# Gate sums of a Mamba-2 mixer: parts made at once, one logarithm, exponential and pair of scalings per group

## The chip, the cores and the metric

The kernel runs on one core of a Trainium2 chip. The core has a matrix engine (TensorE, in the profile PE, with its weight loads as PEld), a vector engine (DVE), an activation engine (ACT), a general engine (POOL) and a queue engine (SP) that issues the transfers. Each engine works through its own list of instructions in order and waits on semaphores. The metric is device time in microseconds; lower is better. Three runs of the kernel before took 2956.16 to 2961.75 us, median 2960.67.

## The reference

One inference step of a hybrid decoder: a Mamba-2 layer, a window-attention layer, each with an MLP, over 1024 prompt rows, 64 sample rows and 16 meta rows (T = 1104 columns here). The change touches the gated norm behind the Mamba-2 scan:

```python
def gated_group_rmsnorm(y, z, w):
    g = (y * jax.nn.silu(z)).astype(jnp.float32)
    shp = g.shape
    g = g.reshape(shp[:-1] + (N_GROUPS, shp[-1] // N_GROUPS))
    g = g * lax.rsqrt(jnp.mean(g * g, axis=-1, keepdims=True) + EPS)
    return (g.reshape(shp) * w.astype(jnp.float32)).astype(y.dtype)
...
    zxbcdt = rmsnorm(h, norm_w) @ w_in
    z = zxbcdt[..., :D_INNER]
...
    out = gated_group_rmsnorm(y, z, gate_w) @ w_out
```

There are 8 groups of 256 features. Each needs z (a product of the normed stream with 256 columns of w_in), the gate, the mean square over its 256 features, its inverse root, and the scaling by that and by w.

## The kernel before

Everything is kept features by rows: 128 partitions hold 128 features, the free dimension runs over the 1104 rows, cut into three chunks of 384, 384 and 336 columns (CH). A group is two tiles of 128 features. Products in full precision are made as three products of rounded parts (mm3, L199 to L206): a number is split into a rounded high part (an ACT copy) and the rest (a subtract).

`gate_group` (L740) makes the gates of one group. It loads two units of weights (wunit, L156: load, ACT cast L170, POOL subtract L171) and the scan's y. For each chunk it makes two products of 24 matrix instructions each; each lands in a bank of PSUM (the matrix engine's output memory; seven banks in this stage). ACT takes the tanh (L754), DVE makes z(1 + tanh) (L755), POOL multiplies by y (L762), ACT squares (L763), DVE adds the two squares (L764). The squares lie in a tile g2 with tag n3, of which there are two.

The sum over the 256 features runs across partitions, so it is a product with a matrix of ones: `sum_over` (L239) splits g2's sum into hi and lo (L249, L250; tiles of tag n1, five of them), multiplies both with ones into one bank (L251, L254) and returns it; `rstd` (L257) takes logarithm (L262) and exponential (L263) of it on ACT, which is the inverse root. `gate_norm` (L776) calls this with rs = the second half of g2, and scales y's two tiles chunk by chunk (L783). After the third chunk `side_sums` (L794) makes sums and differences of the group's quarters on DVE (L800) and stores them (L801, L815) for the block products; groups 6 and 7 are stored as they are (L792).

`gate_norm` isn't called where a chunk's sum is ready. It is put in a list `due` with a count of 3, and `tick` counts down once per product: right after it is put there, after the first product of the next chunk, and after its second. So it is called when the next chunk's products have been written out. Its first product with ones is held behind all matrix instructions written before it (keep_in_program_order, L253). The rest of the order on each engine is fixed at build time by a scheduler that works from its own estimate of times and puts first what it believes ready.

Group 0's gates run inside the last group's scan, groups 1 to 7 in `gates_out` (L822), where one unit of later weights is also split ahead after each group (`split_ahead`, L842: load, split, two stores). When the gates are done, `block_products` (L1216) multiplies the gates with the output weights, in steps p (4 column blocks) and i (7 products each); its raw weights lie in tiles of tag raw for even p and n3 for odd p (L1141). The last chunk of group 7 is still due then: `more` (L855) ticks at p = 0, i = 3 and i = 6, with the ones product in a bank of the block products.

Of the kernel before, what the change touches and what calls it, by code (L numbers as in the profile page):

```python
# [8 lines left out]
F32 = mybir.dt.float32  # L9
F32R = mybir.dt.float32r  # L10
AF = mybir.ActivationFunctionType
ALU = mybir.AluOpType
# [4 lines left out]
P = 128  # L17
D = 1024
# [7 lines left out]
T = META + NM  # L26
# [3 lines left out]
G = 8  # L30
# [12 lines left out]
KB = 3  # L43
# [50 lines left out]
class Stream:  # L94
# [29 lines left out]
    def load(self, X):  # L124

        self.X = X
        for c in self.rs:
            self.k.nc.sync.dma_start(out=X[:, :, self.cols(c)], in_=self.h_d[:, :, self.cols(c)])
        for c in list(self.rs):
            self.norm(c)  # L130
# [11 lines left out]
class Kernel:  # L142
# [96 lines left out]
    def sum_over(self, ssum, n, pin=False):  # L239


        nc = self.nc
        if self.pstat is None:
            ms = self.gps()
        else:
            ms = self.pstat[0].tile([P, self.pstat[3] if len(self.pstat) > 3 else 512], F32, tag=self.pstat[1],
                                    bufs=self.pstat[2], name="ms")
        hi, lo = (self.np.tile([P, 384], F32R, tag="n1", bufs=5, name="ms" + p)[:, :n] for p in "hl")
        nc.scalar.copy(out=hi, in_=ssum)  # L249
        nc.vector.tensor_tensor(out=lo, in0=ssum, in1=hi.bitcast(F32), op=ALU.subtract)  # L250
        a = nc.tensor.matmul(out=ms[:, :n], lhsT=self.ones_r, rhs=hi, start=True, stop=False)  # L251
        if pin:
            self.tc.keep_in_program_order(a)  # L253
        nc.tensor.matmul(out=ms[:, :n], lhsT=self.ones_r, rhs=lo, start=False, stop=True)  # L254
        return ms[:, :n]
# [484 lines left out]
    def gate_group(self, g, xs, y, gt, tmp):  # L740


        nc, i = self.nc, self.i
        w = [self.wunit(self.in_tile(2 * g * P + j * P), KT, P) for j in range(2)]
        for j in range(2):
            nc.sync.dma_start(out=y[j], in_=self.y_d[g][:, j])
        for c, (o, n) in enumerate(CH):
            yv = [t[:, o:o + n] for t in y]
            g2 = gt(c)[:, :, :n]
            for j in range(2):  # L750
                pt = self.gps()
                self.mm3(pt[:, :n], [(w[j][0][:, k], w[j][1][:, k]) for k in range(KT)],
                         [(xs[c][0][:, k, :n], xs[c][1][:, k, :n]) for k in range(KT)])
                nc.scalar.activation(out=g2[:, j], in_=pt[:, :n], func=AF.Tanh, scale=0.5)  # L754
                nc.vector.scalar_tensor_tensor(out=g2[:, j], in0=g2[:, j], scalar=1.0, in1=pt[:, :n],  # L755
                                               op0=ALU.add, op1=ALU.mult)
                if j == 0:
                    self.tick()
                    yield

            for j in range(2):
                nc.gpsimd.tensor_tensor(out=yv[j], in0=g2[:, j], in1=yv[j], op=ALU.mult)  # L762
                nc.scalar.activation(out=g2[:, j], in_=yv[j], func=AF.Square)  # L763
            nc.vector.tensor_tensor(out=g2[:, 0], in0=g2[:, 0], in1=g2[:, 1], op=ALU.add)  # L764
            self.due.append([3, partial(self.gate_norm, g, c, y, g2, tmp)])
            self.tick()
            yield

    def tick(self, n=1):
# [3 lines left out]
        while self.due and self.due[0][0] <= 0:  # L773
            self.due.pop(0)[1]()

    def gate_norm(self, g, c, y, g2, tmp):  # L776
        nc = self.nc
        o, n = CH[c]
        rs = self.rstd(g2[:, 0], n, self.eps4, D / 256, g2[:, 1], pin=True)
        for j in range(2):  # L780
            ft = 2 * g + j
            yv = y[j][:, o:o + n]
            nc.vector.scalar_tensor_tensor(out=yv, in0=yv, scalar=self.nv[:, ft % 8, 6 + ft // 8:7 + ft // 8], in1=rs,  # L783
                                           op0=ALU.mult, op1=ALU.mult)
        if c < 2:
            return
        if g < 2 * KB:
            self.side_sums([t[:, i * T // 2:(i + 1) * T // 2] for t in y for i in range(2)],
                           self.rz[g // KB][:, :, :, g % KB], tmp(), tmp())
        else:  # L790
            for j in range(2):
                nc.sync.dma_start(out=self.gd[g][:, j], in_=y[j])  # L792
# [24 lines left out]
    def gate_of(self, g, xs, yps):  # L817
        y = yps[g % 2].tile([P, 2, T], F32, tag="y", bufs=1, name="gy")
        return self.gate_group(g, xs, [y[:, 0], y[:, 1]], lambda c: self.n3(),
                               lambda: yps[0].tile([P, T // 2], F32, tag="m", bufs=2, name="gm"))  # L820

    def gates_out(self, xs, big, cr, co, cb, yps, gate):  # L822

        nc = self.nc
        nn = T // 2
        ya = yps[1]
        for c, (o, n) in enumerate(CH):
            nc.sync.dma_start(out=big[:, :, o:o + n], in_=self.i["x"][:, :, o:o + n])
        R0 = self.R0 = self.pool("R0", ctx=self.cR, right=True).tile([P, 2, 4, T], F32R, name="R0")
        slot = [P, 2, KB, nn]  # L830
        A5 = self.pool("A5", ctx=co, right=True).tile(slot, F32R, name="A5")
        size = 2 * KB * nn
        cut = lambda t, n: [t[:, k * size:k * size + size].rearrange("p (e q n) -> p e q n", e=2, q=KB)
                            for k in range(n)]
        S = cut(self.S.rearrange("p e k n -> p (e k n)"), 5)
        B = cut(R0.rearrange("p e k n -> p (e k n)"), 2)
        slots = [[[(t[:, 0], t[:, 1])] for t in ts] for ts in ([A5] + B + S[:4], [S[4], A5, A5] + S[:4])]
        load, parts = self.side_io(self.rz, slots)
        for g in range(1, G):
            for _ in gate if g == 1 else self.gate_of(g, xs, yps):  # L840
                pass
            self.split_ahead()  # L842
            if g == 4:
                for i in range(3):
                    load(0, i)
            if g in (5, 6):
                for i in ((0,), (1, 2))[g - 5]:
                    parts(0, i)
        cr.close()
        for i in range(3, 7):  # L850
            load(0, i)
        cb.close()
        us = self.pool("us", ctx=co).tile([P, 4, nn], F32, name="us")

        def more(b, p, i):  # L855
            if (b, p) != (0, 0):
                return
            if 1 <= i <= 4:
                parts(0, i + 2)
            if i in (3, 6):  # L860

                self.pstat = (self.pq, self.CHAIN[0][3], 1, 1024)
                self.tick(2 if i == 3 else 9)
                self.pstat = None
            if i == 6:

                t = ya.tile([P, 4, nn], F32R, tag="y", bufs=1, name="A6")
                rest = self.S.rearrange("p e k n -> p (e k n)")[:, 5 * size:].rearrange("p (q n) -> p q n", q=2)
                slots[1][1] = [(rest, t[:, 0:2]), (t[:, 2:3], t[:, 3:4])]
        self.pq = self.pool("pq", space=PSUM, ctx=co)  # L870
        rd = [self.gd.get(g) for g in range(G)]
        self.block_products(self.i["w_outs"], big, us, slots, load, parts, [(0, 3, 4, 5, 6)], [(3, 6, 7, 8, 10)],
                            (lambda: self.block_load(rd, 3, R0), lambda j: self.block_parts(j, R0)), more, (1, 1))

    def out_last(self, hts, done, norm):
# [1134 lines left out]
```

## Time and profile before

| | |
|---|---|
| runs, median (lowest to highest) | 2960.67 us (2956.16 to 2961.75) |
| the profiled execution | 2959.25 us |
| its span, first to last instruction | 2957.5 us |
| mean granted TensorE clock | 0.982 |
| busy: PE, PEld, DVE | 2829.4, 2719.1, 1888.0 us |
| busy: ACT, POOL | 1454.4, 1370.7 us |
| moved by DMA | 433.44 MB, mean 147 GB/s |

The page's shares are over the whole span; the change is in a stretch of about 300 us (the gates, roughly 600 to 880 us, and the first block products behind them), so that stretch is what has to be read. Busy times of PE are modelled (matrix instructions overlap), so idle time and the pace of products say more than the share. In rows of the order of time the columns are start, duration, engine, line, operation, output<-inputs, shape and count, with the idle time before it and what ended that in brackets. In the list of waits a row has total us, times and the longest.

### The profile page before, as it was taken

To read this page: it belongs to the slowest core of one execution; us is meant where nothing else is said; L and a number is where in the kernel's file an instruction comes from. 1 tells how busy PE (TensorE), PEld (TensorE's weight loads), DVE (VectorE), ACT (ScalarE), POOL (GpSimd) and SP (SyncE) were. 2 spreads that over 40 slices of the span, in tenths; PEclk is the share of its full clock that TensorE was granted. 3 is DMA by queue.
4 is the path that set the end of the run, shared out by engine and by line. 5 is a ranking of instruction groups with operands and counts; after the bars stand their busy time and mean duration, and the time that the engine had idled before them with its cause. 6 is when DMAs were issued, how large, how long until landed. Compare 5 with 4: busy or idle time off the path is not lost.

```text
span 2957.5 us, 51821 instructions
## 1 busy us (share of the span) xinstructions
PE 2829.4 (96%) x19895; PEld 2719.1 (92%) x19895; DVE 1888.0 (64%) x3027; ACT 1454.4 (49%) x2782; POOL 1370.7 (46%) x1279
## 2 busy tenths in 40 slices
PE   8999999989888999999999999999999999999997
PEld 6998999979888999999999999988889999999997
DVE  6788777764645766454547765665678554366675
ACT  6555555556664355545433425555555444433333
POOL 5466666664444714444356663312111444335562
PEclk9999999999998999999999999999999999999999
DMA  3344444447553233444645522447454343543422
GB/s 135 97 131 120 123 125 122 130 136 262 190 199 123 97 113 116 150 140 154 240 166 188 177 79 75 161 152 263 145 187 152 131 156 130 196 161 123 143 99 75
DMA packets 219471, 433.44 MB, mean 147 GB/s; under 512 B 30728, under 2 KB 128392, under 8 KB 216648
## 3 DMA queue, kind: packets, MB, share of 16 engines
q1 hardware_dynamic: 219224, 430.14, 43.7%
q8 instruction: 156, 2.56, 0.4%
q14 instruction: 91, 0.75, 0.1%
HBM read 302.71 MB, written 128.32 MB: 146 GB/s over the span
## 4 chain that ended last, share of the span: by engine, by line
PE 59%; DVE 7%; ACT 4%; issue 4%; DMA 3%; POOL 3%; SPq 0%; DVEq 0%; ACTq 0%; POOLq 0%
PE g L204 6%; PE g L206 6%; PE g L205 6%; PE mc L204 4%; PE mc L205 3%; PE mc L206 3%; PE ma L204 3%; PE ma L205 3%; PE ma L206 3%; PE md L206 3%; PE md L205 3%; PE mb L204 3%; PE mb L206 3%; PE md L204 3%; PE mb L205 3%
## 5 line engine op out<-in xcount | busy, mean ns | idle before, releaser
L1031 POOL TENSOR_TENSOR w<-s,w 128x384 fp32r<-128x384 f32 (+1 forms) x272 | 364.8, 1347 | 421.7 <-ACT w L1030 386.0
L204 PE MATMUL g<-S,w 128*128 128x384 f32 (+2 forms) x1584 | 535.2, 338 | 2.2 <-ACT w L170 0.8
L206 PE MATMUL g<-S,w 128*128 128x384 f32 (+2 forms) x1584 | 532.8, 337 | 3.4 <-POOL w L171 2.7
L205 PE MATMUL g<-S,w 128*128 128x384 f32 (+2 forms) x1584 | 535.2, 338 | 0.0
L1031 POOL TENSOR_TENSOR w<-raw,w 128x384 fp32r<-128x384 f32 (+1 forms) x204 | 262.1, 1290 | 278.5 <-ACT w L1030 247.7
L171 POOL TENSOR_TENSOR w<-raw,w 128x1024 fp32r<-128x1024 f32 x96 | 243.8, 2541 | 273.6 <-ACT w L170 211.8
L206 PEld LDWEIGHTS g<-S,w 128*128 128x128 f32 x1584 | 303.7, 192 | 5.2 <-POOL w L171 3.0
L204 PEld LDWEIGHTS g<-S,w 128*128 128x128 f32 x1584 | 302.9, 191 | 5.9 <-issue 1.6
L205 PEld LDWEIGHTS g<-S,w 128*128 128x128 f32 x1584 | 303.7, 192 | 0.9 <-issue 0.3
L1030 ACT CAST w<-s 128x384 fp32r<-128x384 f32 (+1 forms) x272 | 150.0, 557 | 302.4 <-DVE s L1155 70.6
L204 PE MATMUL ma<-S,w 128*128 128x276 f32 (+1 forms) x808 | 236.2, 292 | 9.3 <-DVE us L1247 6.7
L205 PE MATMUL ma<-S,w 128*128 128x276 f32 (+1 forms) x808 | 235.5, 292 | 2.3 <-DVE S L1213 2.3
L206 PE MATMUL ma<-S,w 128*128 128x276 f32 (+1 forms) x808 | 235.6, 292 | 0.0
L1030 ACT CAST w<-raw 128x384 fp32r<-128x384 f32 (+1 forms) x204 | 112.2, 556 | 161.9 <-PE md L206 46.1
L594 DVE SCALAR_TENSOR_TENSOR fm<-xp,cv,fm 128x1024 f32<-128x1024 f32 x96 | 161.2, 1681 | 33.0 <-ACT fm L575 32.4
L204 PEld LDWEIGHTS ma<-S,w 128*128 128x128 f32 x808 | 154.4, 191 | 10.8 <-ACT w L1030 4.8
L205 PE MATMUL g<-R,w 128*128 128x384 f32 (+2 forms) x480 | 158.3, 330 | 0.0
L204 PE MATMUL g<-R,w 128*128 128x384 f32 (+2 forms) x480 | 157.8, 329 | 0.0
L206 PE MATMUL g<-R,w 128*128 128x384 f32 (+2 forms) x480 | 157.7, 329 | 0.0
L205 PEld LDWEIGHTS ma<-S,w 128*128 128x128 f32 x808 | 154.6, 191 | 2.5 <-DVE S L1213 2.5
L206 PEld LDWEIGHTS ma<-S,w 128*128 128x128 f32 x808 | 154.2, 191 | 0.0
L204 PE MATMUL mc<-S,w 128*128 128x276 f32 (+1 forms) x512 | 149.5, 292 | 4.7 <-DVE rx L1060 2.4
(491 smaller groups left out, 8679.3 us busy)
## 6 DMA issues: line engine op xcount, KB each, us to landing
raw<-in_w_up_dram SPq DMA_DIRECT2D x64, 512.0 KB
raw<-in_w_in_dram SPq DMA_DIRECT2D x48, 512.0 KB
raw<-in_w_downs_dram SPq DMA_DIRECT2D x64, 384.0 KB
w<-ws_o SPq DMA_DIRECT2D x48, 512.0 KB
w<-ws_q SPq DMA_DIRECT2D x40, 512.0 KB
ab<-acs_d SPq DMA_DIRECT2D x64, 256.0 KB
S<-t_d SPq DMA_DIRECT2D x18, 828.0 KB
S<-t_e SPq DMA_DIRECT2D x18, 816.0 KB
```

The costliest lines, as they stand in the source:

```text
L171: nc.gpsimd.tensor_tensor(out=wl, in0=raw, in1=wh.bitcast(F32), op=ALU.subtract)
L204: mm(out=out, lhsT=wh, rhs=xh, start=(first and k == 0), stop=False)
L205: mm(out=out, lhsT=wh, rhs=xl, start=False, stop=False)
L206: mm(out=out, lhsT=wl, rhs=xh, start=False, stop=(k == n - 1))
L594: nc.vector.scalar_tensor_tensor(out=acc[:, :SEQ], in0=xp[:, k:k + SEQ], scalar=cv[:, j, k:k + 1], in1=acc[:, :SEQ], op0=ALU.mult, op1=ALU ...
L1030: nc.scalar.copy(out=t[:, 0], in_=src)
L1031: nc.gpsimd.tensor_tensor(out=t[:, 1], in0=src, in1=t[:, 0].bitcast(F32), op=ALU.subtract)
```

## The change

- `sum_over` is cut in two: `sum_parts` makes hi and lo, `sum_of` makes the products with ones.
- `gate_group` calls `sum_parts` right where a chunk's sum is ready, after the tick, and puts `gate_norm` in the list with a count of 2, without a tick behind it; so the products with ones still come when the next chunk's products have been written out. For group 0's first two chunks it is called at once.
- `gate_norm` copies the sums of a chunk into its columns of one rs tile for the group (ACT). After the third chunk there is one logarithm, one exponential and two scalings over all 1104 columns. The halves of rs serve `side_sums` as its two temporary tiles.
- That tile is the only one of its tag, in the pool that stays open over the block products; before there were two half-wide ones in the other pool.
- After the last group nothing is split ahead. The unit is split later, in the first MLP's block products (L1189).
- The last chunk's tick in the block products is at i = 5, not 3; the tick at i = 6 goes.

```diff
     def sum_over(self, ssum, n, pin=False):
+        return self.sum_of(self.sum_parts(ssum, n), n, pin)
+
+    def sum_parts(self, ssum, n):
+        nc = self.nc
+        hi, lo = (self.np.tile([P, 384], F32R, tag="n1", bufs=5, name="ms" + p)[:, :n] for p in "hl")
+        nc.scalar.copy(out=hi, in_=ssum)
+        nc.vector.tensor_tensor(out=lo, in0=ssum, in1=hi.bitcast(F32), op=ALU.subtract)
+        return hi, lo
+
+    def sum_of(self, parts, n, pin):
...
-        hi, lo = (self.np.tile([P, 384], F32R, tag="n1", bufs=5, name="ms" + p)[:, :n] for p in "hl")
-        nc.scalar.copy(out=hi, in_=ssum)
-        nc.vector.tensor_tensor(out=lo, in0=ssum, in1=hi.bitcast(F32), op=ALU.subtract)
+        hi, lo = parts
...
             nc.vector.tensor_tensor(out=g2[:, 0], in0=g2[:, 0], in1=g2[:, 1], op=ALU.add)
-            self.due.append([3, partial(self.gate_norm, g, c, y, g2, tmp)])
             self.tick()
+            parts = self.sum_parts(g2[:, 0], n)
+            self.due.append([2, partial(self.gate_norm, g, c, y, parts, tmp)])
+            if g == 0 and c < 2:
+                self.tick(2)
             yield
...
-        rs = self.rstd(g2[:, 0], n, self.eps4, D / 256, g2[:, 1], pin=True)
+        if c == 0:
+            self.grs = tmp()
+        rs = self.grs
+        nc.scalar.copy(out=rs[:, o:o + n], in_=self.sum_of(parts, n, g > 0 or c == 2))
+        if c < 2:
+            return
+        nc.scalar.activation(out=rs, in_=rs, func=AF.Ln, bias=self.eps4, scale=D / 256)
+        nc.scalar.activation(out=rs, in_=rs, func=AF.Exp, scale=-0.5)
         for j in range(2):
             ft = 2 * g + j
-            yv = y[j][:, o:o + n]
-            nc.vector.scalar_tensor_tensor(out=yv, in0=yv, scalar=self.nv[:, ft % 8, 6 + ft // 8:7 + ft // 8], in1=rs,
-                                           op0=ALU.mult, op1=ALU.mult)
-        if c < 2:
-            return
+            nc.vector.scalar_tensor_tensor(out=y[j], in0=y[j], scalar=self.nv[:, ft % 8, 6 + ft // 8:7 + ft // 8],
+                                           in1=rs, op0=ALU.mult, op1=ALU.mult)
...
-                           self.rz[g // KB][:, :, :, g % KB], tmp(), tmp())
+                           self.rz[g // KB][:, :, :, g % KB], rs[:, :T // 2], rs[:, T // 2:])
...
-                               lambda: yps[0].tile([P, T // 2], F32, tag="m", bufs=2, name="gm"))
+                               lambda: yps[1].tile([P, T], F32, tag="m", bufs=1, name="gm"))
...
-            self.split_ahead()
+            if g < G - 1:
+                self.split_ahead()
...
-            if i in (3, 6):
+            if i == 5:
                 self.pstat = (self.pq, self.CHAIN[0][3], 1, 1024)
-                self.tick(2 if i == 3 else 9)
+                self.tick(9)
                 self.pstat = None
```

More of the change, by code (lines that the diff above doesn't have):

```diff
@@ L774, in tick, with gate_norm @@
             self.due.pop(0)[1]()
-    def gate_norm(self, g, c, y, g2, tmp):
+    def gate_norm(self, g, c, y, parts, tmp):
         nc = self.nc
         o, n = CH[c]
-        rs = self.rstd(g2[:, 0], n, self.eps4, D / 256, g2[:, 1], pin=True)
+        if c == 0:
[6 more added lines that the diff above has]
+        nc.scalar.activation(out=rs, in_=rs, func=AF.Exp, scale=-0.5)
         for j in range(2):
             ft = 2 * g + j
-            yv = y[j][:, o:o + n]
-            nc.vector.scalar_tensor_tensor(out=yv, in0=yv, scalar=self.nv[:, ft % 8, 6 + ft // 8:7 + ft // 8], in1=rs,
-                                           op0=ALU.mult, op1=ALU.mult)
-        if c < 2:
-            return
+            nc.vector.scalar_tensor_tensor(out=y[j], in0=y[j], scalar=self.nv[:, ft % 8, 6 + ft // 8:7 + ft // 8],
+                                           in1=rs, op0=ALU.mult, op1=ALU.mult)
         if g < 2 * KB:
             self.side_sums([t[:, i * T // 2:(i + 1) * T // 2] for t in y for i in range(2)],
-                           self.rz[g // KB][:, :, :, g % KB], tmp(), tmp())
+                           self.rz[g // KB][:, :, :, g % KB], rs[:, :T // 2], rs[:, T // 2:])
         else:
```

## The prediction

> **What bounds the kernel now.** I read the page first (share of each engine), then the list of waits of PE for the stretch where the gates run, then busy time by stage, then the order of time of one group.
>
> ```profile
> span 2957.5 us, 51821 instructions
> ...
> PE 2829.4 (96%) x19895; PEld 2719.1 (92%) x19895; DVE 1888.0 (64%) x3027; ACT 1454.4 (49%) x2782; POOL 1370.7 (46%) x1279
> ```
> ```profile
> PE ms L254 <- DVE msl L250: 15.2, 8, 3.0
> PE mb L204 <- ACT w L1030: 7.8, 1, 7.8
> PE ms L251 <- ACT msh L249: 11.0, 9, 3.0
> ...
> PE ma L205 <- DVE S L1213: 2.3, 1, 2.3
> ...
> PE g L251 <- ACT msh L249: 2.1, 1, 2.1
> PE ma L204 <- ACT S L1212: 1.3, 1, 1.3
> ```
> ```profile
> 661.40:877.30 215.90, 192.48 (x1050) 186.47 (x1050) 112.14 (x155) 142.10 (x206) 100.30 (x67) 0.94 0.59 210
> 877.30:925.00 47.70, 31.89 (x187) 30.07 (x187) 29.07 (x36) 27.41 (x40) 17.91 (x14) 0.79 0.50 185
> 925.00:980.00 55.00, 53.89 (x419) 53.19 (x418) 39.25 (x43) 24.27 (x34) 33.66 (x26) 1.00 0.45 154
> ```
>
> TensorE is the bound, so only what makes it wait is worth time. The second fence (600 to 960 us) says who makes it wait there: the products with ones (L251, L254) wait for the two parts of a chunk's sum (ACT copy L249, DVE subtract L250). The third fence holds the gates of groups 1 to 7, the entry into the block products, and a quiet stretch to compare with; columns are PE, PEld, DVE, ACT, POOL busy, granted clock, DMA share, GB/s. ACT is busy 142.10 of 215.90 us: not the bound.
>
> How much PE loses, from the pace of its products:
>
> ```profile
> L204 PE MATMUL g<-S,w 128*128 128x384 f32 x224 | 78.7, 351 | 0.0
> ...
> L204 PE MATMUL g<-S,w 128*128 128x336 f32 x112 | 36.1, 322 | 0.0
> ```
> ```profile
> 721.33 0.34 PE L206 MATMUL g<-S,w 128*128 128x384 f32 x1
> ...
> 730.46 0.33 PE L204 MATMUL g<-S,w 128*128 128x384 f32 x1
> ...
> 773.54 0.31 PE L204 MATMUL g<-S,w 128*128 128x336 f32 x1
> ...
> 780.79 0.32 PE L206 MATMUL g<-S,w 128*128 128x336 f32 x1
> ...
> 786.85 0.69 PE L254 MATMUL ms<-msl,ones_r 128*128 128x384 f32 x1 [2.33 <-DVE msl L250]
> 787.34 0.52 PE L205 MATMUL g<-S,w 128*128 128x384 f32 x1
> 787.66 0.52 PE L206 MATMUL g<-S,w 128*128 128x384 f32 x1
> ...
> 790.21 0.34 PE L205 MATMUL g<-S,w 128*128 128x384 f32 x1
> ```
>
> 53 products of 384 columns run from 721.33 to 730.46: 9.13/52 = 0.176 us each; 48 of 336 from 773.54 to 780.79: 7.25/47 = 0.154. In the gates' stretch L204, L205 and L206 have 224 + 112 each, so 672 x 0.176 + 336 x 0.154 = 170.0 us; the 42 ones products that remain of the 1050 take another 28 x 0.176 + 14 x 0.154 = 7.1. Elapsed 215.9, so **38.8 us are lost**. The named waits are 15.2 + 11.0 + 2.1 less one of 3.0 that comes after 877.3, less 2.1 just before 661.4: 23.2. The clock, 0.94, accounts for 0.06 x 215.9 = 13.0: behind the wait at 786.85 the products follow at 0.32 us (787.34 to 787.66), not 0.176, and nine of them take 2.87 us up to 790.21 in place of 1.58. Waits and the slow clock behind them make 36.2 of 38.8.
>
> Here trace and the Trainium skill differ. Its page "TensorE: Matmul & The Clock Gate" (HAM oscillation) puts the abstract rule as no idle gaps of PE over about 3.4 us; in this trace gaps of at most 3.0 us are followed by slow products. By the page's rule these short gaps should leave the clock alone, and the 13.0 would not come back: the gain below would be smaller by up to that. I go by the rows.
>
> The second stretch: 183 block products (187 less 4 ones) at 55.00/419 = 0.131 us are 24.0, ones 0.7: of 47.7 us, **23.0 lost**. Waits there: 3.0 for c1's parts, 7.8 for weights, 2.3 and 1.3 for the S parts.
>
> **The change, part by part.** One group's chain, where the waits come from:
>
> ```profile
> 783.84 2.54 POOL L171 TENSOR_TENSOR w<-raw,w 128x1024 fp32r<-128x1024 f32 x1
> ...
> 784.10 2.70 DVE L250 TENSOR_TENSOR msl<-n,msh 128x384 fp32r<-128x384 f32 x1
> ...
> 787.85 0.56 DVE L250 TENSOR_TENSOR msl<-n,msh 128x384 fp32r<-128x384 f32 x1 [0.58 <-ACT msh L249]
> ```
> ```profile
> 801.02 0.87 ACT L754 ACTIVATE n<-g 128x384 f32<-128x384 f32 x2 [0.98 <-DVE gy L783]
> ...
> 802.30 0.42 PE L251 MATMUL ms<-msh,ones_r 128*128 128x336 f32 x1 [1.03 <-ACT msh L249]
> ...
> 803.59 0.42 PE L254 MATMUL ms<-msl,ones_r 128*128 128x336 f32 x1 [0.18 <-DVE msl L250]
> ...
> 804.99 1.28 ACT L262 ACT_TABLE_LOAD   x1
> ...
> 806.28 0.54 ACT L262 ACTIVATE n<-ms,eps 128x336 f32<-128x336 f32 x1
> 806.84 1.28 ACT L263 ACT_TABLE_LOAD   x1
> ...
> 808.13 0.48 ACT L263 ACTIVATE n<-n 128x336 f32<-128x336 f32 x1
> 808.73 1.05 DVE L783 SCALAR_TENSOR_TENSOR gy<-gy,nv,n 128x336 f32<-128x336 f32 x2 [3.17 <-ACT n L263]
> ...
> 813.08 0.32 SPq L801 DMA_DIRECT2D z_d<-gm  x1
> ```
>
> Row 801.02 is the key: a tanh waits for L783 of two chunks before. The square tile (tag n3, 2 buffers) also holds rs, so it comes free only after logarithm, exponential and scaling. So parts -> ones -> Ln -> Exp -> scaling -> tanh -> parts is a ring through two buffers, with 2 x 1.28 us of table loads in it, and PE waits on it once or twice a group.
>
> *Parts at once.* No instruction is added; copy and subtract run right behind the chunk's sum, about one chunk (48 x 0.176 = 8.4 us) before PE asks. Even the slow subtract (2.70 beside POOL's 2.54, otherwise 0.56) fits. The square tile is free then, so the ring is cut. Behind the copy on ACT stand the next tanh and the weight casts; PSUM holds seven product banks, over 28 us of products, so such a delay does not reach PE. Held longer are four of the five n1 buffers, of which side_sums and the block's weight sums use the rest.
>
> *One Ln and Exp.* Per group ACT loses four table loads (5.1 us) and four narrow activations, and gains three copies of about 0.54 and two wide ones. A wide one is L597's 1.13 us. Some 4.5 us of ACT less a group; ACT is not the bound, so alone worth 0.
>
> *Two scalings for six.* The same elements; 1104 columns by L594 take 1.681 x 1104/1024 = 1.81 us.
>
> ```profile
> L594 DVE SCALAR_TENSOR_TENSOR fm<-xp,cv,fm 128x1024 f32<-128x1024 f32 x96 | 161.2, 1681 | 33.0 <-ACT fm L575 32.4
> ```
> ```profile
> L597 ACT ACTIVATE th<-fm 128x1104 f32<-128x1104 f32 x1 | 1.1, 1126 | 1.4 <-DVE fm L594 1.4
> ```
> ```profile
> 729.21 2.06 DMA z_d<-gy
> ```
>
> *What is late next.* rs is now one tile for all groups, and its halves go out as side_sums' m and u. The next group's first copy waits until they have landed, and behind it the single ones bank. Before, from 802.30 to the store's landing: 813.08 + 0.32 + 2.06 - 802.30 = 13.2 us. After: -1.1 (the second ones product no longer lags 1.29), +0.54 copy, +0.6 Ln, +0.65 Exp, +2.6 scalings (2 x 1.81 for 1.05), and 0.54 for the waiting copy: 17.0. PE reaches the ones product that needs the bank after two chunks and their ones, 8.4 + 7.4 + 0.7 = 16.5. So PE waits 0.5 us a group, 3.5 for seven, a gap far shorter than the 2.33 at 786.85, so I add no slow clock. Behind the waiting copy on ACT stand tanhs and part copies, unless the scheduler puts them first; behind the waiting ones product stand all later products. Another 1 us a group I leave for the scheduler's order, which is fixed at build time. Lower end 0; upper end when both wide scalings meet POOL as the L250 above did: 2 x 2.14 more, 4.8 of wait and 2.87 - 1.58 = 1.3 of slow clock, 6.1 x 7 = 43, all of the gain. The Trainium skill, "SBUF — State Buffer" (Who interferes with whom), says why: a DVE operation with two SBUF inputs and a GpSimd one exclude each other for the whole instruction; the 2.70 agrees, and a rule so read speaks against wide scalings. **Gates: 38.8 - 3.5 - 7 = 28 gained** (-4 to 39).
>
> *Stores on SP* go out some 3 us later, and with them the y and weight loads queued behind. The list of PE's waits names no DMA in this stretch: 0, at most 3 a group.
>
> *The end.* The 7.8 us wait is for weights whose raw tile needs an n3 buffer:
>
> ```profile
> SPq L1143 <- DVE gy L783: 2.9, 1, 2.9
> ```
> ```profile
> 909.08 1.05 DVE L783 SCALAR_TENSOR_TENSOR gy<-gy,nv,n 128x336 f32<-128x336 f32 x2 [3.35 <-ACT n L263]
> ```
> ```profile
> 910.57 0.81 SPq L1143 DMA_DIRECT2D raw<-in_w_outs_dram  x1
> ```
>
> The raw load at 910.57 waits for L783 of the last chunk at 909.08. With the parts made at once the buffer is free before any ones product, and 7.8 goes, as do the 3.0 and about 5 of slow clock behind both (0.21 x 47.7 = 10.0 in all). What stays are the S parts (2.3 + 1.3), whose loads cannot start before the gates' last product: 23.0 - 7 = **16 gained** (8 to 21). The last chunk's tick moves from i = 3 to 5; nobody on PE waits for its result within the stretch; its cover is the weights' head start on SP, and if the stores stood before those loads it would cost up to the same 7.8 again. The wait of 2.1 before 661.4 (group 0's second chunk, whose ones now come at once) goes too: **2**.
>
> *The split skipped for the last group* runs in a later block instead: one POOL subtract of about 2.5 us beside PE. The seven like it there have no PE wait of their own: 0, at most the longest wait of that stage.
>
> ```profile
> PE mb L204 <- DVE hh L1247: 4.8, 1, 4.8
> ```
>
> Sum: 28 + 16 + 2 = **46 us**. The profiled execution took 2959.25 (its span 2957.5), 1.4 below the median of the runs, 2960.67; so 2913 by the former and **2915** by the median.
>
> **The rivals.** *The gain is halved*: PE no longer waits for parts but for the ones bank, 2 to 3 us a group, with 1.3 of slow clock behind: 7 x 3.8 = 27 of the 39 stay, and 2960.7 - 12 - 18 = 2931. For it: 17.0 against 16.5 is a tie. Chance 0.22. *It doesn't do what it says*: the planned order puts copies so late on ACT that the gates lose as much as now, and only the end gains: 2960.7 - 18 = 2943; chance 0.07. *Slower*: the ring through the single rs tile. Every us by which its chain passes 16.5 costs PE 7; it decides from 16.5 + 57/7 - 1.3 = about 23.3 us, where 57 is the gain without it (39 + 16 + 2). With both scalings blocked I get 21.3, still 2960.7 - 57 + 43 = 2947; two more blocked DVE operations (side_sums, 2.1 each) make 25.6, that is 7 x (25.6 - 16.5 + 1.3) = 73, a time of 2977. Against it: 13.2 is seen today with the same neighbours. Chance 0.06. *Everything goes*: 39 + 21 + 2 = 62, 2899; chance 0.1.
>
> **How the numbers follow.** The forecast's case, 2902 to 2926, has 0.55. The range 2896 to 2941 takes in the halved gain and most of the full one, and leaves out about 0.15. Within 0.2% (5.9 us, about what this kernel's runs can tell apart) I put 0.03, slower 0.06, faster 0.91.
>
> **What would show it.** Right: PE's waits on L250 and L249 in the gates gone or under 1 us; granted clock near 1.00 there; about 27 us a group (177/7 and 1.5), not 215.9/7 = 31; L254 directly behind L251; the tanh no longer waiting for L783; two table loads a group; no 7.8 us wait on the first block's weights. Wrong: ones products waiting for the copy out of their bank (ACT), with L783 far over 1.8 us; or PE waiting on PSUM banks or on w.

## The result and the profile after

The changed kernel took 2931.05 us (median of 4 runs, 2929.05 to 2932.74) against 2958.41 for the kernel before beside it: ratio 0.9909, 95% interval 0.9891 to 0.9926, so 27 us less where 46 were forecast. The profiled execution took 2932.74 us.

The page's first lines, then PE's waits from 590 to 960 us (total us, times, longest), then busy time by stage (length, busy us and count of PE, PEld, DVE, ACT and POOL, granted clock, DMA share, GB/s):

```profile
span 2930.7 us, 51725 instructions
...
PE 2814.7 (96%) x19895; PEld 2710.2 (92%) x19895; DVE 1899.7 (65%) x2995; ACT 1413.4 (48%) x2742; POOL 1381.0 (47%) x1279
```
```profile
PE ms L262 <- DVE msl L248: 14.2, 5, 5.2
PE md L204 <- ACT w L1048: 6.1, 1, 6.1
PE ms L259 <- ACT msh L247: 3.4, 2, 2.5
PE md L206 <- POOL w L1049: 1.7, 1, 1.7
...
PE ms L259 <- ACT gm L795: 1.1, 1, 1.1
```
```profile
661.40:865.20 203.80, 185.15 (x1046) 182.31 (x1047) 117.42 (x135) 109.48 (x172) 103.72 (x69) 0.96 0.61 215
865.20:905.00 39.80, 31.79 (x223) 31.04 (x223) 31.64 (x30) 23.29 (x33) 25.36 (x17) 0.87 0.55 199
```

In the changed kernel hi and lo are L247 and L248, the ones products L259 and L262, the copy out of the ones bank L795. The gates' stretch, up to their last product, is 203.80 us where it was 215.90: 12.1 less, not 28. ACT's busy time there fell from 142.10 to 109.48. But the ones products still wait for the parts, 14.2 + 3.4 us in place of 15.2 + 11.0 + 2.1 (3.0 of it after the gates). The wait of 7.8 us on weights of the block's second step is gone, and one of 6.1 + 1.7 on weights of its first step stands in its place.

Start of PE's n-th matrix instruction in the two executions, counted out of the traces:

```
n       before     after   difference
3600     560.8     563.6     +2.8
4000     620.9     627.8     +6.9
4400     696.9     695.8     -1.1
4800     780.0     778.2     -1.8
5200     868.2     855.9    -12.3
5600     945.0     920.2    -24.8
6000     997.9     974.0    -23.9
13600   2077.0    2053.1    -23.9
15200   2317.8    2290.3    -27.5
```

The +2.8 is scatter: nothing has changed up to there, and the executions of the runs below, alike up to that instruction, reach it at 560.2 to 563.2. Group 0's gates inside the scan cost 4 and give 8 back, groups 1 to 7 give 11, the entry into the block products 12. The stretch with the moved split gives and costs nothing. A last 3.6 appears behind instruction 13600. The execution before takes 240.9 us from there to 15200, the change's 237.3 and the runs below 235.6 to 238.2, so that it may be scatter too; its cause is open.

What the one logarithm and exponential removed shows in ACT's groups of the gates' stretch, first of the kernel before, then of the changed one (count, busy us, mean ns, idle before):

```profile
L262 ACT ACT_TABLE_LOAD x21 | 26.9, 1283 | 0.4
L263 ACT ACT_TABLE_LOAD x21 | 26.9, 1283 | 0.4
```
```profile
L798 ACT ACT_TABLE_LOAD x7 | 9.0, 1283 | 0.1
...
L799 ACT ACT_TABLE_LOAD x5 | 6.4, 1283 | 0.1
...
L762 ACT ACT_TABLE_LOAD x2 | 2.6, 1283 | 0.0
```

42 loads became 14; twice the second load is that of a tanh which slipped between logarithm and exponential. Where the waits now come from is one place in the order of time:

```profile
738.24 2.65 DVE L802 SCALAR_TENSOR_TENSOR gy<-gy,nv,gm 128x1104 f32<-128x1104 f32 x2 [1.49 <-ACT gm L799]
...
741.27 0.73 DVE L817 TENSOR_TENSOR gm<-gy 128x552 f32<-128x552 f32 x1
...
741.43 1.44 POOL L770 TENSOR_TENSOR gy<-n,gy 128x384 f32<-128x384 f32 x1 [5.09 <-DVE n L763]
...
742.03 1.43 DVE L817 TENSOR_TENSOR gy<-gy 128x552 f32<-128x552 f32 x1
...
742.83 2.41 POOL L168 TENSOR_TENSOR raw<-raw,nv 128x1024 f32<-128x1024 f32 x1
...
743.34 0.50 ACT L247 CAST msh<-n 128x384 fp32r<-128x384 f32 x1
...
743.38 2.45 DVE L817 TENSOR_TENSOR gm<-gy,gm 128x552 f32<-128x552 f32 x1
...
746.22 1.58 DVE L817 TENSOR_TENSOR o<-gy,gm 128x276 f32<-128x276 f32 x2
...
747.46 2.54 POOL L171 TENSOR_TENSOR w<-raw,w 128x1024 fp32r<-128x1024 f32 x1
...
747.73 2.69 DVE L248 TENSOR_TENSOR msl<-n,msh 128x384 fp32r<-128x384 f32 x1
...
750.47 0.69 PE L262 MATMUL ms<-msl,ones_r 128*128 128x384 f32 x1 [4.38 <-DVE msl L248]
```

Hi is there at 743.84, but lo stands on DVE behind the group before's two scalings and its side sums, a burst of 9.5 us (738.24 to 747.73, with two small operations of other chunks in it), and then runs 2.69 us where 0.56 is usual, beside POOL's 2.54. PE waits 4.38. The burst is itself stretched beside POOL: its three subtracts of 128x552 take 0.73, 1.43 and 2.45 us, the last one beside POOL's 2.41 (742.83). The Trainium skill, "SBUF — State Buffer" (Who interferes with whom), has a DVE operation with two SBUF inputs shut out by a GpSimd one that reads SBUF; the row agrees: lo ends 0.42 us behind POOL's subtract (750.42 and 750.00).

### The profile page after: what moved, and what is told of

The parts are those of the page before. It is cut to its first block, busy times and chain, and to the rows that moved or that the text cites. A ratio compares the mean times of both kernels' runs of the same rounds, so it can differ in the third digit from the quotient of the medians.

```text
span 2930.7 us, 51725 instructions
## 1 busy us (share of the span) xinstructions
PE 2814.7 (96%) x19895; PEld 2710.2 (92%) x19895; DVE 1899.7 (65%) x2995; ACT 1413.4 (48%) x2742; POOL 1381.0 (47%) x1279
## 4 chain that ended last, share of the span: by engine, by line
PE 75%; DVE 9%; DMA 4%; issue 4%; ACT 4%; POOL 3%; SPq 0%; DVEq 0%; POOLq 0%; ACTq 0%
PE g L204 10%; PE g L205 10%; PE g L206 10%; PE mc L204 3%; PE mc L206 3%; PE mc L205 3%; PE ma L204 3%; PE ma L206 3%; PE ma L205 3%; PE md L206 2%; PE mb L206 2%; PE mb L204 2%; PE md L205 2%; PE mb L205 2%; PE md L204 2%
```

## The experiments

All were timed in five rounds beside the kernel before, whose medians were 2955.34 to 2959.26 us; the change itself was timed once, so two runs are compared best by their ratios to the kernel before. The trace of a run is of one execution, which is not always near the median. The first theories were two. Theory 1: the DVE burst above is the reason why the gates gave 12 and not 28. Theory 2: the parts, held longer, keep n1 tiles from the block's first weights, which is why the end gave 12 and not 16. The rivals were the prediction's: the single ones bank and rs tile, and a saving on ACT that counts after all.

### Parts traced ahead of the scalings (e1_parts_first)

```diff
-            self.tick()
             parts = self.sum_parts(g2[:, 0], n)
+            self.tick()
```

> A chunk's sum and its two parts are traced ahead of the waiting scalings of the group before (sum_parts before tick in gate_group), nothing else changes. Theory 1 (the low part of chunk 0 stands on VectorE behind the group before's two wide scalings and side sums, 1.49 to 2.82 us each, and PE's ones product waits for it: L262 <- L248, 14.2 us in 5 waits): those waits fall below 4 us in sum and the run comes to 2913 to 2920 us, 11 to 18 less than the change's 2931. Rival A (the single ones bank and the single rs tile hold the ones products, so that the order on VectorE does not matter): 2928 to 2934, the waits move from L262 to L259 or to the bank's copy. Rival B (the scalings, put off, hold the gates of the next group or the side sums' stores): the waits on L248 go, and as many us come back at L763, L770 or at the block's loads: 2928 to 2934.

Measured: 2937.64 us (2932.38 to 2940.52), ratio 0.9925 (0.9912 to 0.9939). Not faster than the change. PE's waits, 661.4 to 870 us:

```profile
PE ms L259 <- ACT gm L795: 9.8, 4, 3.4
PE ms L262 <- DVE msl L248: 4.9, 4, 2.5
PE ms L259 <- ACT msh L247: 4.4, 3, 1.6
```

The waits moved as rival A said: 19.1 us in sum, where the change has 14.2 + 3.4 + 1.1 = 18.7. With lo out of the way, the copy out of the bank is late, since it goes into the rs tile that the side sums still use: in the gates ACT stands idle 4.9 us ahead of it for L817, where in the change it stood idle 0.3 in all. Theory 1 named the place, but the time that it gave did not come.

### Group 7's second chunk at once (e2_c1_now)

```diff
-            if g == 0 and c < 2:
+            if (g == 0 and c < 2) or (g == G - 1 and c == 1):
                 self.tick(2)
...
-self.sum_of(parts, n, g > 0 or c == 2)
+self.sum_of(parts, n, (g > 0 or c == 2) and not (g == G - 1 and c == 1))
```

> The ones products of group 7's chunk 1 are made as soon as its parts are there, and not pinned into program order, so that the two n1 tiles of its parts come free some 8 us earlier. Theory 2 (the first weights of the block wait for n1 tiles that hold parts: PE waits 6.1 us on L1048 and 1.7 us on L1049 at 874 to 877): the two waits fall to 2 us or less in sum and the run comes to 2923 to 2927. Rival (the sums of those weights stand behind the S parts and the low part of chunk 2 in VectorE's order in any case, so the tiles are not what is late): the waits stay over 5 us in sum, 2929 to 2934.

Measured: 2931.97 us (2931.42 to 2932.68), ratio 0.9906 (0.9893 to 0.9920): the rival. The waits on the block's first weights were 8.4 and 1.8 us. But in PE's order the first of the two ones products came just ahead of the gates' last product instead of just behind it, not some 8 us earlier, so this edit did not free the tiles, and it says nothing against theory 2.

### Two ones banks (e3_two_banks)

```diff
-                self.more_banks(cr, 4)
+                self.more_banks(cr, 3, 2)
```

> Two banks for the ones products in place of one, three in place of four for the gate products. Theory 1 (VectorE's order): no gain, 2930 to 2935, since only 1.1 us of PE's waits are for the bank's copy by ScalarE (L259 <- L795), and three product banks may cost some. The prediction's rival (the loop through the one ones bank and the one rs tile): 8 us or more less, 2916 to 2923.

Measured: 2937.28 us (2936.07 to 2937.72), ratio 0.9924 (0.9911 to 0.9936): slower than expected by theory 1 and far from the rival's 2916 to 2923. The wait on the bank's copy is gone, but the waits on L248 were 14.7 us, about as in the change, and those on hi rose from 3.4 to 5.3. A second ones bank that takes no bank from the gate products was not run.

### A logarithm and exponential for each chunk (e4_ln_each)

```diff
-        if c < 2:
-            return
-        nc.scalar.activation(out=rs, in_=rs, func=AF.Ln, bias=self.eps4, scale=D / 256)
-        nc.scalar.activation(out=rs, in_=rs, func=AF.Exp, scale=-0.5)
+        part = rs[:, o:o + n]
+        nc.scalar.activation(out=part, in_=part, func=AF.Ln, bias=self.eps4, scale=D / 256)
+        nc.scalar.activation(out=part, in_=part, func=AF.Exp, scale=-0.5)
+        if c < 2:
+            return
```

> One logarithm and exponential for each chunk on its slice of rs, in place of one for the group; the wide scalings, the early parts and the rest stay. It gives back four table loads of 1.28 us a group and the small activations' fixed cost, some 8 to 9 us of ScalarE a group. If ScalarE's savings alone are worth nothing, as predicted (ScalarE busy 109.5 of 203.8 us in the gates): 2930 to 2935. Rival (the single logarithm and exponential are where the gain is): 2941 to 2952.

Measured: 2950.55 us (2945.52 to 2953.76), ratio 0.9966 (0.9954 to 0.9979). The rival: by the medians 19.5 of the change's 27 us are gone, by the ratios 17 (0.9966 against 0.9909), and the waits on the parts are up to 28.5:

```profile
PE ms L262 <- DVE msl L248: 15.8, 6, 6.8
PE ms L259 <- ACT msh L247: 12.7, 9, 3.1
```

This overturned the prediction's price of nothing for the one logarithm and exponential, and led to theory 3: what stands in ACT's queue is what counts.

### Early parts alone (e5_early_only)

The kernel before, with `sum_parts` and `sum_of` and

```diff
-            self.due.append([3, partial(self.gate_norm, g, c, y, g2, tmp)])
             self.tick()
+            parts = self.sum_parts(g2[:, 0], n)
+            self.due.append([2, partial(self.gate_norm, g, c, y, parts, g2[:, 1], tmp)])
+            if g == 0 and c < 2:
+                self.tick(2)
```

> The kernel before with the parts made at once and the ones products two products later, and no other part of the change (a logarithm, an exponential and two scalings for each chunk stay, rs stays in the chunk's square tile, the split ahead stays). First theory of the prediction (the ring through the square tile and the late parts are the loss, ScalarE's savings are worth nothing): parts early give half or more of the 28 us, 2938 to 2948. Theory 3 (a chunk's chain goes through ScalarE in order five times, and the 3.7 us of table loads, logarithm and exponential that stand in it for each chunk are what delays it, as the 19 us of the run with a logarithm for each chunk say): parts early alone gain little, 2950 to 2962.

Measured: 2952.01 us (2947.68 to 2956.81, 11 runs), ratio 0.9981 (0.9973 to 0.9990). Theory 3: parts at once gain about 5.6 us here. In this kernel rs stays in the square tile, so the ring of the prediction is not cut; the run above, with rs in a tile of its own, has both halves of that step.

### All but early parts (e6_parts_late)

```diff
-            parts = self.sum_parts(g2[:, 0], n)
-            self.due.append([2, partial(self.gate_norm, g, c, y, parts, tmp)])
+            self.due.append([2, partial(self.gate_norm, g, c, y, g2, tmp)])
...
         o, n = CH[c]
+        parts = self.sum_parts(g2[:, 0], n)
```

> The change with the parts made late again, in gate_norm just ahead of their ones products; one logarithm, one exponential and two wide scalings a group, and rs in its own tile, stay. Prediction's theory (late parts make PE wait about 3 us in a chunk): most of the gain is gone, 2945 to 2960. Theory 3 (ScalarE's fewer instructions carry most of it): half or more of the 28 us stays, 2932 to 2945.

Measured: 2926.75 us (2921.93 to 2933.36), ratio 0.9893 (0.9875 to 0.9910): below even theory 3's range. Without the early parts nothing of the gain is lost. The reason shows in the two traces side by side: from 661 us to about 860 DVE, ACT and POOL run the same instructions in the same order in both, and PE waits alike (this run, 640 to 920 us):

```profile
PE ms L262 <- DVE msl L248: 14.6, 5, 5.2
PE ms L259 <- ACT msh L247: 3.3, 2, 2.4
PE md L204 <- ACT w L1048: 2.0, 1, 2.0
PE ma L204 <- DVE hh L1265: 1.2, 1, 1.2
PE ms L259 <- ACT gm L795: 1.1, 1, 1.1
```

The scheduler puts hi and lo in the same place whether they are written early or late. The orders part only where the block begins. There the early parts do harm: the sums of the first weights (L1167) run at 860.06 us here, and at 872.83 in the change, and the block's wait is 2.0 in place of 6.1 + 1.7. Of the 5.2 us between the spans of the two traces this is only a part: 3.4 are there at instruction 3600, where the kernels are still alike.

### Parts first and two banks (e7_first_two)

Both edits of the first and third experiment.

> Parts ahead of the waiting scalings, together with two ones banks (three product banks). Theory 4 (two waits in series: with the parts first, the waits go from L248, 14.2 us, to the copy of the one bank, L795, 9.8 us, because that copy goes to the one rs tile that the side sums still hold; a second bank lets the ones products go on without the copy): waits on L248 and L795 in sum under 6 us, and 2915 to 2926. Rival (the bank is not what holds, or three product banks cost as much as they cost alone, 6 us): 2931 to 2940.

Measured: 2934.28 us (2929.56 to 2936.75), ratio 0.9915 (0.9900 to 0.9930): the rival, in time. The waits on L248 and the bank's copy fell to 4.5 as expected, and the waits on hi rose to 15.0. Two answers of this run, PE's waits and ACT's idle time before the bank's copy:

```profile
PE ms L259 <- ACT msh L247: 15.0, 6, 4.5
...
PE ms L262 <- DVE msl L248: 4.5, 4, 1.6
```
```profile
L247 ACT CAST msh<-n 128x384 fp32r<-128x384 f32 (+1 forms) x20 | 9.9, 497 | 16.6 <-DVE n L772 16.6
L795 ACT COPY gm<-ms 128x384 f32<-128x384 f32 (+1 forms) x20 | 9.1, 458 | 8.0 <-DVE o L817 6.1 <-PE ms L262 1.5 <-DMA z_d<-gm 0.3
```

ACT itself now stands still for the side sums (L817, 6.1 us) ahead of the copy, and hi waits for the squares' sum (L772), which is behind the same burst on DVE. Again 19.5 us in sum.

### Without the side sums' subtractions (e8_no_subs)

The gates' side sums (five subtract instructions a group; the expectation says six) leave the subtractions out and store what lies in the tiles, so the kernel does less than the computation and gives a bound.

> The change without the six subtractions of the gates' side sums: the stores send the rows as they are, so part of the computation is left out. Bound on what VectorE's burst behind the scalings costs. Theory 1 and 4 (that burst holds both the low part of chunk 0 and the rs tile): waits on L248 fall by 8 us or more, and 2915 to 2924. Rival (the burst fills time that the next link of the chain would wait in anyway): waits fall by less than 4 us, 2927 to 2933.

Measured: 2919.50 us (2917.85 to 2927.12), ratio 0.9873 (0.9854 to 0.9892); 11.5 less than the change by the medians, 11 by the ratios. This edit took waits on the parts away rather than moving them; those on the block's first weights (L1065, L1066) stayed. Waits of 661.4 to 870 us, then the gates in two stretches (their last product is at 850.4), then products behind a wait:

```profile
PE md L204 <- ACT w L1065: 6.8, 1, 6.8
PE ms L259 <- ACT msh L247: 6.5, 7, 2.1
PE ms L262 <- DVE msl L248: 3.9, 4, 2.1
PE md L206 <- POOL w L1066: 1.3, 1, 1.3
```
```profile
661.40:780.00 118.60, 111.75 (x633) 109.18 (x632) 61.35 (x65) 65.94 (x103) 67.52 (x42) 0.97 0.74 263
780.00:850.00 70.00, 66.46 (x389) 64.98 (x389) 27.25 (x38) 40.58 (x66) 30.50 (x23) 1.00 0.47 167
```
```profile
712.63 0.44 PE L259 MATMUL ms<-msh,ones_r 128*128 128x384 f32 x1 [2.09 <-ACT msh L247]
...
714.36 0.53 PE L204 MATMUL g<-S,w 128*128 128x384 f32 x1
714.68 0.53 PE L205 MATMUL g<-S,w 128*128 128x384 f32 x1
```

In the first stretch, with two waits of 2.1 us, the granted clock is 0.97: behind the one at 712.63 the products follow at 0.32 us. In the second no wait is over 1.1 us, and the clock is 1.00.

### The table loads alone (e9_tables)

```diff
         if c < 2:
+            if g > 1:
+                nc.scalar.activation(out=self.one, in_=rs[:, o:o + 1], func=AF.Ln, bias=self.eps4, scale=D / 256)
+                nc.scalar.activation(out=self.one, in_=self.one, func=AF.Exp, scale=-0.5)
             return
```

> The change, with the two table loads put back for the first two chunks of groups 2 to 7: a logarithm and an exponential of one column each, on a tile of their own, just behind the copy of the bank; their results are used by nothing. So 24 loads of 1.28 us and 24 activations of one column, but nothing of the scalings waits for them. Theory 3a (the loads' time in ScalarE's queue, between a chunk's tanh, squares and high part, is what the single logarithm and exponential saved): 10 to 20 us slower than the change, 2941 to 2951, with waits on L247 and L248 up by 6 us or more. Theory 3b (what counts is that the scalings, the small logarithm and exponential themselves and the tiles they hold are done once): within 4 us of the change, 2928 to 2935.

Measured: 2946.08 us (2945.05 to 2951.68, 8 runs), ratio 0.9967 (0.9957 to 0.9977). Theory 3a: by the medians 15.0 us, by the ratios 17 (0.9967 against 0.9909), for 24 loads of 1.28 us and 24 activations of one column, though PE was still the busiest engine in the gates and ACT far from it (139.50 of 211.80 us, PE 186.57). Waits on hi rose from 3.4 to 8.6, on lo from 14.2 to 16.1, so by 7.1 in sum, and the block's first weights waited 8.0 + 1.7 where it was 6.1 + 1.7. The trace is of the slowest of the eight executions (2951.68 us); in it the gates are 8.7 us longer than in the change's trace, and the products behind them, up to instruction 6000, 2.8. The rest was not followed. How a pair stands in ACT's order:

```profile
825.64 1.28 ACT L798 ACT_TABLE_LOAD   x1
826.94 0.29 ACT L798 ACTIVATE one<-gm,eps 128x1 f32<-128x1 f32 x1
827.25 1.28 ACT L799 ACT_TABLE_LOAD   x1
828.54 0.20 ACT L799 ACTIVATE one<-one 128x1 f32<-128x1 f32 x1
828.65 0.47 ACT L762 ACTIVATE n<-g 128x384 f32<-128x384 f32 x1
```

For 3.0 us no tanh, square, hi or cast can run. The Trainium skill, "ScalarE: Activation LUTs" (Table sets: the hidden batching unit), gives the rule: batch activation calls by table set. This run and the one with a logarithm for each chunk agree, with 15.0 and 19.5 us by the medians. Their ratios are the same (0.9967 and 0.9966), so what the logarithms and exponentials of the chunks cost beyond the loads is not shown.

### Side sums spread (e10_spread) and the last group's parts late (e11_spread_late)

The first two subtractions are traced one product behind the scalings, the other three two products behind:

```diff
-            self.side_sums([t[:, i * T // 2:(i + 1) * T // 2] for t in y for i in range(2)],
-                           self.rz[g // KB][:, :, :, g % KB], rs[:, :T // 2], rs[:, T // 2:])
+            steps = self.side_steps([t[:, i * T // 2:(i + 1) * T // 2] for t in y for i in range(2)],
+                                    self.rz[g // KB][:, :, :, g % KB], rs[:, :T // 2], rs[:, T // 2:])
+            self.due += [[1, partial(next, steps)], [2, partial(next, steps)]]
```

> The change with the gates' side sums traced in two steps, one and two products behind the wide scalings, in place of at once; all work stays. Theory 4 (VectorE's burst behind the scalings holds chunk 0's low part: without the subtractions the run was 11.5 us faster): the low part now goes ahead of most of the burst, waits on L248 fall from 14.2 to under 6 us; but the rs tile is held longer, so some comes back at the bank's copy (L795): 2920 to 2928. Rival (as with the parts put first: what L248 gives, L795 takes): 2929 to 2938.

Measured: 2936.27 us (2928.86 to 2937.72), ratio 0.9931 (0.9917 to 0.9945): the rival. L248 3.5, hi 4.8, the bank's copy 12.0: 20.3 in sum.

The second kernel also makes the parts of group 7 in `gate_norm`.

> The same spread side sums, and the parts of the last group made late, just ahead of their ones products, so that they hold no n1 tiles when the block's first weights are summed. Theory 2 (early parts keep n1 tiles from the block's first weights; with late parts for all groups the run was 4 us faster and the wait at the block's start was 2.0 in place of 7.8 us): 4 to 6 us less than the run with spread side sums alone, and waits on the block's first weights of 3 us or less. Rival (the 4 us came from elsewhere in the gates): equal to the spread run within 2 us.

Measured: 2935.77 us (2932.76 to 2936.50), ratio 0.9931 (0.9919 to 0.9944). The waits, with the copy again at 11.0:

```profile
PE md L206 <- POOL w L1076: 2.2, 1, 2.2
PE md L204 <- ACT w L1075: 1.5, 1, 1.5
```

Theory 2 is right about the wait: 3.7 us where the spread kernel has 6.6 + 1.3. The time is the same within 2 us, as the rival has it, so what this wait is worth is not shown: single runs of either kernel lie 4 to 9 us apart.

### Late parts, three of the subtractions on POOL (e12_pool)

```diff
+        sub = lambda out, x, y: (last or nc.vector).tensor_tensor(out=out, in0=x, in1=y, op=ALU.subtract)
         sub(u, r[3], m)
```

with nc.gpsimd as `last` for the gates, on top of the kernel with late parts.

> The change with its parts made late (the run that came to 2926.75 us) and with the last three of the five subtractions of each gates' side sums on GpSimd in place of VectorE: VectorE's burst is shorter by about 3.4 us a group, all work stays. Theory 4b (it is the length of VectorE's burst that counts, not its order: without the subtractions 11.5 us were gained, with the parts put first or the sums spread nothing was): two thirds or so of that come, 2916 to 2923, and waits on L248 under 9 us. Rival (GpSimd's share comes back, as the gate products L770 and the cast parts L171 stand behind it there, and the two engines slow one another): 2925 to 2935.

Measured: 2924.90 us (2921.98 to 2926.34), ratio 0.9893 (0.9876 to 0.9909). Just below the rival's range: the same ratio as with late parts alone. Waits on the parts fell from 17.9 to 15.0, and PE waits anew for POOL's subtract of the weights (last row):

```profile
PE ms L262 <- DVE msl L248: 9.9, 6, 2.9
PE ms L259 <- ACT msh L247: 5.1, 2, 3.2
PE g L206 <- POOL w L171: 1.6, 3, 1.1
```

It and the kernel with late parts have the lowest ratios of those that do all the work. Their intervals reach into the change's, 0.9891 to 0.9926, so that they beat the change is not shown; that they beat the kernel before is. In the traces the gates take 198.4 us in this run and 204.0 in the change and with late parts, which the times do not show.

## Why the prediction was right in its number and wrong in its reasons

The two edits that the argument is about, as ratios to the kernel before:

| | parts late | parts at once |
|---|---|---|
| logarithm for each chunk | 1 | 0.9981 (rs in the square tile), 0.9966 (own rs tile, wide scalings) |
| one for the group | 0.9893 | 0.9909 (the change) |

The kernel with late parts and one logarithm has the own rs tile and the wide scalings too. Down a column the ratio falls by 0.006 to 0.011, along a row by 0.002 to 0.003 at the top and not at all at the bottom. The traces say the same by stretch (one execution of each kernel; gates are counted from PE's instruction 4208 to the gates' last product, the block from there to instruction 6000):

| us | gates | block |
|---|---|---|
| before | 215.8 | 120.6 |
| early parts alone | 212.3 | 122.6 |
| the change | 204.0 | 109.2 |
| the change, parts late | 204.0 | 106.1 |
| the change, logarithm for each chunk | 216.9 | 112.0 |
| the change, table loads put back | 212.7 | 112.0 |
| the change, no subtractions | 193.2 | 108.3 |

- *"Parts at once", the term of 28: this step failed.* It held that copy and subtract would run one chunk earlier. In the gates they run where the scheduler puts them anyway; with late parts the order there is the same. Alone they were worth 5.6 us, and in the change nothing that can be measured (204.0 us both ways). With a logarithm for each chunk, where the parts are early and rs is out of the square tile, so that the ring is cut as the prediction has it, the gates are no shorter than before. That the square tile comes free before the exponential is so (no tanh waits for a scaling), but the tanh then waits for lo: ACT's L762 behind L248, 13.5 us in four waits.
- *"One Ln and Exp ... alone worth 0": this step failed too, the other way.* The reason given was that ACT is not the bound. Busy share was the wrong measure. A chunk passes ACT five times in order (two tanhs, two squares, hi), and PE asks for its parts one chunk later, by the prediction's own 8.4 us. Whatever stands in that queue delays the later links. That this chain is the way is argued from the order; the price is measured. Putting 24 loads back, with activations of one column, costs 15.0 us by the medians, a logarithm and exponential for each chunk 19.5; by the ratios both cost 17.
- *The bank and rs loop, 17.0 against 16.5:* forecast 3.5 us, 1.1 measured. The term was about right in the change, because lo was later still. The half-gain rival gave 2931, the time that came, by the mechanism of this loop; that mechanism was not what halved the gain here, but it took over in each run that put lo forward with one ones bank (9.8, 12.0 and 11.0 us).
- *Wide scalings at 1.81 us each:* 2.65 us for two, so 1.33 (738.24); over the fourteen of the gates' stretch the mean is 1.61, the longest 2.76. What they cost alone was not run. What was not costed is that with the five subtractions behind them they form one burst in front of the next group's lo.
- *The end, 16:* mis-sized, about 12 (-12.3 to -24.8 between instructions 5200 and 5600). The 7.8 went as argued, but the sentence "side_sums and the block's weight sums use the rest" (the tiles not held by parts) was too light: a wait of 6.1 + 1.7 on the first weights took its place. That early parts cause it is shown by the runs with late parts (2.0, and 1.5 + 2.2); that it is by the tiles that they hold is argued. With late parts the block's stretch is 14.5 us shorter than before, near the 16, and the change's 11.4; by instruction 8000 the two differ by 0.9, no longer by 3.1, so what the wait costs in the end is not settled.
- *Group 0's wait, 2, and the moved split, 0:* in the table of instructions group 0's gates cost 4 and give 8; the split shows no cost (-23.9 at instruction 6000 and at 13600).
- *The clock:* 0.96, not 1.00, since most waits stayed. That short waits can cost clock, the side that the prediction took against the Trainium skill's page "TensorE: Matmul & The Clock Gate" (HAM oscillation), held: without the subtractions products at 0.32 us follow a wait of 2.09. Not every short wait does it: in the change's trace the products behind one of 2.83 us (784.55) follow at 0.17 to 0.18.

So the gain is 27 us, not 46, and that the time lies in the stated range is luck in its main part: of the gates' 28 us about 12 came, and they came from the edit priced at nothing, while the edit priced at 28 gave none. What stays open: why the sum of waits is 18.7 to 20.9 us in every order that was tried. The runs show that it falls with the work in DVE's burst (6.5 + 3.9 = 10.4 without the subtractions, 9.9 + 5.1 + 1.4 = 16.4 with three of them on POOL), not with its order. Whether by the burst's length, by the time for which it holds the rs tile or by its meeting POOL was not separated. What each order trades for what beyond the rows above was not followed, nor was a second rs tile tried.

## What to carry to other kernels

An engine that is idle half of the time can still set the pace, if one item passes it several times in order: price what stands in its queue against the slack of that chain, not against its busy share. Before crediting an edit with moving instructions earlier, compare the order on each engine; a scheduler may have put them there already. And where waits only change their names as things are put forward, look for the work that all of them stand behind, and take that away.

## What was unexpected of the hardware

A table load took 1.28 us each time, and the next activation began within 0.02 us (825.64 + 1.28 to 826.94). The Trainium skill, "ScalarE: Activation LUTs" (What ACT_TABLE_LOAD costs), adds a drain of some 1.38 us to each switch; no row here shows one. A DVE subtract of 128x552 took 0.73 us where it began ahead of POOL's product (741.27 and 741.43), and 1.43 where the next one began behind it (742.03). And the runs of some orders lie further apart than those of others: 2928.86 to 2937.72 with the side sums spread, against 2931.42 to 2932.68 with group 7's second chunk at once; why is open.
